# Transposed tokens in tiles of 512, streamed 512 at a time in three products

## The chip, the core and the metric

The kernel runs on one core of a Trainium2 chip. Its time is the device time of that core in microseconds. Three timed runs gave 2494.58, 2495.59 and 2495.97 us; the median is 2495.59 us. The engines are TensorE (PE, with its weight loads shown as PEld), VectorE (DVE), ScalarE (ACT), GpSimd (POOL) and SyncE (SP), which issues all DMAs here.

## The reference

One encoder layer is computed for two request groups with shared weights: S (512 tokens) and R (1024 tokens), both 1024 wide.

```
u = rmsnorm(x, mix_norm_g) @ w_in            # columns: z 512, xbc 1024, dt 16, q 512, k 512, v 512
ssd_out = ssd_mixer(z, xbc, dt)              # conv over tokens, two chunked scans, gate, norm
att_out = attention_mixer(q, k, v)           # dilated attention, three patterns
h = x + concat(ssd_out, att_out) @ w_out
h = h + memory_cross_attention(rmsnorm(h), rmsnorm(mem))      # 4 heads of 256, 256 memory tokens
hm = rmsnorm(h, mlp_norm_g)
return h + jnp.square(jax.nn.relu(hm @ mlp_w1)) @ mlp_w2      # 1024 -> 4096 -> 1024
```

All of it is float32. The kernel keeps that precision by splitting each operand of a large product into a high and a low part and summing three products.

## The kernel before

**Normed, transposed tokens.** Before each projection two token tiles of 128 are normed, transposed on PE into PSUM (`to_T`, L199) and written out by ACT as the high part `chi` (L205) and by DVE as the low part `clo` (L206). `at_pair` allots the two tiles, each 128 partitions by 8 slices `k` of the model width by 256 tokens. The pools `atA` and `atB` hold four such tiles each, so two pairs. `norm_T` and `to_T` fill a pair slice by slice.

**Products.** `mm3` (L181 to L183) issues three matmuls for one slice: high by high, low by high, high by low. In a matmul the first argument is the stationary operand, which is loaded as weights, and the second one streams. Two forms of product use the pairs:

- *Token-major* (`proj`): 128 tokens are stationary and 256 columns of a weight slab stream. Query, key and value, the gates, `w_out`, the memory's keys and values and the cross-attention's queries have this form. In the trace their matmuls read `mm<-whi,chi`: the streaming operand stands first.
- *Channel-major*: 128 columns of the weights are stationary and tokens stream, 256 at a time. This is `ch_major` in `w_in` (the 1024 conv channels), the time steps `steps` (32 columns of weights), and `up` in `mlp`, the feed-forward's first product. In the trace: `mm<-chi,whi`, `mm<-chi,wds` and `tp<-chi,whi`. A PSUM tile holds 512 tokens, so each of these runs 8 slices for the first pair of a block of 512 tokens and then 8 for the second.

**Feed-forward.** `up(fb)` makes 256 hidden channels (two groups `ft` of 128) for each block of 512 tokens: S has one block, R two. `down(fb)` multiplies them by 256 rows of `w2`, streaming 512 columns per matmul (`mm<-whi,hidh`), and adds to `h` on DVE (L947). There are 16 `fb`. `up(fb + 1)` is written ahead of `down(fb)`.

**Stages.** S: `w_in`, its scan `ssd`, its q, k and v. Then S's attention runs beside R's `w_in`, R's scan beside R's q, k and v, and R's attention beside S's `w_out`, cross-attention (`xattn`) and feed-forward. Last come R's `w_out`, cross-attention and feed-forward, with nothing beside them. `chain` holds the last three steps: `hn` norms a pair for the cross-attention and `hm` one for the feed-forward as soon as the pair's `h` is complete.

**What sets the order.** The source order isn't the order on the engines: a list scheduler places every instruction by its own estimate of when its operands are ready. On each engine the placed order is then fixed; an instruction whose operand isn't ready holds up those behind it. Dependences are kept by the parts of a tile that are read and written, and a pool's buffer is given on when its whole tile has been read.

Of the kernel before, what the change touches and what calls it, by code (L numbers as in the profile page):

```python
# [11 lines left out]
F32R = mybir.dt.float32r  # L12
# [8 lines left out]
KT = D // 128  # L21
# [63 lines left out]
def encoder(ctx: ExitStack, tc: tile.TileContext, I, y_p, y_s):  # L85
    nc = tc.nc
# [137 lines left out]
    def at_pair(atp):  # L224

        return tuple(atp.tile([128, KT, 256], F32R, name=n, tag="c8") for n in ("chi", "clo"))

    class Stream:
        def __init__(self, tag, x, mem, y, T):
            self.tag, self.x, self.mem, self.y, self.T = tag, x, mem, y, T  # L230
            self.nt = T // 128
            self.at, self.mixT, self.h, self.hn, self.hm = [], [], [], [], []
# [15 lines left out]
    def proj(w, hl, t):  # L248

        ps = mm_bank()[:, 0:256]  # L250
        (hi, lo), (wh, wl) = hl, w
        ts = slice(t * 128, t * 128 + 128)
        for k in range(KT):
            mm3(ps, hi[:, k, ts], lo[:, k, ts], wh[:, k, :], wl[:, k, :], k == 0, k == KT - 1)
        return ps


    def w_in_norm(st, pool, atp, b, first=None):

        for pr in range(2):  # L260
# [11 lines left out]
            st.at.append(at_pair(atp))  # L272
            norm_T(xs, *st.at[-1], "mix_norm_g", pool, more_banks if first else (tp_bank,))

    def w_in(st, pool, wx, first=False):
# [5 lines left out]
        def ch_major(ps, w, c, b):  # L281
            wh, wl = w
            cs = slice(c * 128, c * 128 + 128)
            for pr in range(2):
                hi, lo = at[b * 2 + pr]
                pp = ps[:, pr * 256:pr * 256 + 256]
                for k in range(KT):
                    mm3(pp, wh[:, k, cs], wl[:, k, cs], hi[:, k, :], lo[:, k, :], k == 0, k == KT - 1)
# [43 lines left out]
        def gate(c):  # L332
            w = slab(W_IN, OFF_Z + c * 256)
            for t in range(0, nt, 2):
                th = pool.tile([128, 512], F32, name="ev").rearrange("p (t c) -> p t c", t=2)
                for i in range(2):
                    ps = proj(w, at[t // 2], i)
# [6 lines left out]
        def steps(_):  # L344
# [8 lines left out]
            for b in range(nb):  # L353
                pd = mm_bank()
                for pr in range(2):
                    hi, lo = at[b * 2 + pr]
                    pp = pd[:32, pr * 256:pr * 256 + 256]
                    for k in range(KT):
                        nc.tensor.matmul(pp, wds[:, k, :], hi[:, k, :], start=k == 0, stop=False)
                        nc.tensor.matmul(pp, wds[:, k, :], lo[:, k, :], start=False, stop=k == KT - 1)  # L360
# [42 lines left out]
    def w_in_qkv(st, pool, rot, mid=None):  # L403
# [37 lines left out]
        for c in range(6):  # L441
            w = slab(W_IN, OFF_Q + c * 256)
            for t in range(0, nt, 2):
                hl = [pool.tile([128, 512], F32R, name="ev") for _ in range(2 if c < 4 else 1)]
                e = f(hl[-1]).rearrange("p (t c) -> p t c", t=2)
                for i in range(2):
                    ps = proj(w, st.at[t // 2], i)
# [279 lines left out]
    def memory_norm(pool, atp):  # L727
        for st in (S, R):
# [5 lines left out]
            st.mt = at_pair(atp)  # L734
            norm_T(xs, *st.mt, "mem_norm_g", pool)

    def memory(pool, late=None):
        for c in range(8):
# [3 lines left out]
            for st in (S, R):  # L742
                kf = pool.tile([128, 512], F32, name="ev").rearrange("p (m c) -> p m c", m=2)
                ss = pool.tile([128, 2], F32, name="kss", bufs=2)
                for mt in range(2):
                    ps = proj(w, st.mt, mt)
# [24 lines left out]
    def mix_T(st, pr, atp, banks=(tp_bank,)):  # L771
# [8 lines left out]
        st.mixT.append(at_pair(atp))  # L780
        to_T(xs, *st.mixT[-1], lambda k: gcol("ssd_norm_g", k), banks,
             lambda k: ident if k < 4 else back)

    def norm_h(st, pr, atp, gname, banks):
        hl = at_pair(atp)
# [265 lines left out]
```

## Time and profile before

| | |
|---|---|
| median of three timed runs | 2495.59 us |
| the profiled execution's own time | 2489.01 us |
| its span | 2487.2 us |
| PE busy | 2419.2 us (97%) |
| PEld busy | 2268.0 us (91%) |
| DVE, ACT, POOL busy | 1394.9, 951.3, 698.4 us |
| matmuls recorded | 17363 |
| mean granted TensorE clock | 0.993 of full speed |

Durations of matmuls overlap: one is shown from its start until its modelled end, while the next one has begun. So the rate of a stream is read from starts, not from durations. PE's idle time in a row is the time before an instruction in which no matmul was under way, with what ended it.

### The profile page before, as it was taken

The numbers are of one execution on the slowest core, as the hardware profiler recorded it, in microseconds if no ns is written. First come the engines' busy times: TensorE is split into PE (matmuls) and PEld (weight loads), VectorE is DVE, ScalarE is ACT, GpSimd is POOL, SyncE is SP. The second block draws the span as 40 slices with busy tenths as digits, with TensorE's granted clock in tenths as the row PEclk, the third lists the DMA queues.
The fourth block names the chain that finished last, engine by engine and source line by source line (L and its number), as shares of the span: only waits on it lengthen the run. The fifth ranks groups of instructions, "written<-read, shape, count | busy, mean of one in ns | idle before, by whom it ended". The sixth has DMA issues, their size and how long they took to land.

```text
span 2487.2 us, 43450 instructions
## 1 busy us (share of the span) xinstructions
PE 2419.2 (97%) x17363; PEld 2268.0 (91%) x17363; DVE 1394.9 (56%) x2750; ACT 951.3 (38%) x2153; POOL 698.4 (28%) x492
## 2 busy tenths in 40 slices
PE   8989999999989999999999999999999999999999
PEld 8889999889889988999989999999989989989897
DVE  6896775787735666655445636445544444443444
ACT  6655554455544655543222315334412212112120
POOL 3363112564422221314334211111222222122220
PEclk9999999999999999999999999999999999999999
DMA  5755443765567253425233411111111111101101
GB/s 187 243 192 181 126 146 106 225 201 189 187 194 214 85 150 98 116 83 184 92 101 103 170 52 35 52 60 44 35 52 35 51 52 51 52 35 52 52 35 68
DMA packets 224059, 272.59 MB, mean 110 GB/s; under 512 B 39634, under 2 KB 178160, under 8 KB 223856
## 3 DMA queue, kind: packets, MB, share of 16 engines
q1 hardware_dynamic: 223856, 269.80, 34.1%
q8 instruction: 137, 2.24, 0.4%
q14 instruction: 66, 0.54, 0.1%
HBM read 215.55 MB, written 54.20 MB: 108 GB/s over the span
## 4 chain that ended last, share of the span: by engine, by line
PE 79%; DMA 6%; DVE 6%; issue 3%; POOL 2%; ACT 2%; SPq 1%; POOLq 0%; DVEq 0%; ACTq 0%
PE mm L181 16%; PE mm L183 16%; PE mm L182 16%; PE tp L183 7%; PE tp L182 7%; PE tp L181 7%; PE mc L676 2%; PE ma L653 2%; PE mb L666 1%; DMA se<-acp 1%; DVE wlo L173 1%; PE tp L199 1%; DVE se L558 1%; POOL wlo L173 1%; DMA ak<-qkp 1%
## 5 line engine op out<-in xcount | busy, mean ns | idle before, releaser
L181 PE MATMUL mm<-whi,chi 128*128 128x256 f32 x1792 | 516.6, 289 | 2.1 <-ACT mm L749 1.2
L183 PE MATMUL mm<-whi,clo 128*128 128x256 f32 x1792 | 512.2, 287 | 0.0
L182 PE MATMUL mm<-wlo,chi 128*128 128x256 f32 x1792 | 511.3, 286 | 0.0
L947 DVE TENSOR_TENSOR h<-mm,h 128x512 f32<-128x512 f32 x384 | 262.2, 689 | 408.6 <-PE mm L183 408.6
L173 POOL TENSOR_TENSOR wlo<-raw,whi 128x1024 fp32r<-128x1024 f32 x120 | 296.9, 2474 | 601.4 <-ACT whi L172 585.9
L183 PE MATMUL tp<-chi,wlo 128*128 128x256 f32 x1440 | 408.4, 284 | 0.0
L182 PE MATMUL tp<-clo,whi 128*128 128x256 f32 x1440 | 407.9, 283 | 0.0
L181 PE MATMUL tp<-chi,whi 128*128 128x256 f32 x1440 | 405.6, 282 | 0.0
L172 ACT CAST whi<-raw 128x1024 fp32r<-128x1024 f32 x240 | 241.7, 1047 | 293.1 <-PE mm L183 168.1
L181 PEld LDWEIGHTS mm<-whi,chi 128*128 128x128 f32 x1792 | 341.1, 190 | 4.5 <-ACT chi L205 1.7
L182 PEld LDWEIGHTS mm<-wlo,chi 128*128 128x128 f32 x1792 | 341.0, 190 | 1.2 <-issue 0.2
L183 PEld LDWEIGHTS mm<-whi,clo 128*128 128x128 f32 x1792 | 339.9, 190 | 0.4
L173 DVE TENSOR_TENSOR wlo<-raw,whi 128x1024 fp32r<-128x1024 f32 x120 | 265.8, 2215 | 108.5 <-ACT whi L172 108.2
L181 PE MATMUL mm<-whi,hidh 128*128 128x512 f32 x768 | 303.1, 395 | 0.2 <-DVE h L947 0.2
L182 PE MATMUL mm<-wlo,hidh 128*128 128x512 f32 x768 | 302.6, 394 | 0.0
L183 PE MATMUL mm<-whi,hidl 128*128 128x512 f32 x768 | 302.3, 394 | 0.2 <-POOL hidl L932 0.2
L181 PEld LDWEIGHTS tp<-chi,whi 128*128 128x128 f32 x1440 | 272.5, 189 | 8.7
L183 PEld LDWEIGHTS tp<-chi,wlo 128*128 128x128 f32 x1440 | 271.7, 189 | 7.0
L182 PEld LDWEIGHTS tp<-clo,whi 128*128 128x128 f32 x1440 | 270.9, 188 | 6.5
L932 POOL TENSOR_TENSOR hidl<-hr,hidh 128x512 fp32r<-128x512 f32 x96 | 133.3, 1390 | 473.6 <-ACT hidh L931 473.6
L931 ACT CAST hidh<-hr 128x512 fp32r<-128x512 f32 x96 | 59.5, 620 | 320.6 <-PE mm L182 249.6
L183 PEld LDWEIGHTS mm<-whi,hidl 128*128 128x128 f32 x768 | 144.3, 188 | 34.0 <-POOL hidl L932 0.6
(283 smaller groups left out, 4398.3 us busy)
## 6 DMA issues: line engine op xcount, KB each, us to landing
raw<-in_mlp_w_dram SPq DMA_DIRECT2D x128, 512.0 KB
raw<-in_w_in_dram SPq DMA_DIRECT2D x48, 512.0 KB
qkp<-ev SPq DMA_DIRECT2D x32, 256.0 KB
se<-acp SPq DMA_DIRECT2D x16, 512.0 KB
raw<-in_xatt_wkv_dram SPq DMA_DIRECT2D x16, 512.0 KB
ak<-qkp SPq DMA_DIRECT2D x32, 256.0 KB
raw<-in_w_out_dram SPq DMA_DIRECT2D x16, 512.0 KB
raw<-in_xatt_wq_dram SPq DMA_DIRECT2D x16, 512.0 KB
```

The costliest lines, as they stand in the source:

```text
L172: nc.scalar.copy(hi[:, sl, :], raw)
L173: (nc.vector if s else nc.gpsimd).tensor_tensor(lo[:, sl, :], raw, f(hi[:, sl, :]), op=OP.subtract)
L181: nc.tensor.matmul(ps, lh, rh, start=start, stop=False)
L182: nc.tensor.matmul(ps, lh, rl, start=False, stop=False)
L183: nc.tensor.matmul(ps, ll, rh, start=False, stop=stop)
L199: nc.tensor.transpose(pt[:, k, t, :], xn[t][:, (2 * kp + k) * 128:(2 * kp + k + 1) * 128], units(2 * kp + k))
L558: nc.vector.scalar_tensor_tensor(w[:, h], cbm[:, 0, g], col[2], w[:, h], op0=OP.mult, op1=OP.add)
L653: nc.tensor.matmul(pq[:, i, :W], qu, ops[i][0][j], start=j == 0, stop=j == 1)
L676: nc.tensor.matmul(po[:, i * 64:i * 64 + 64], pT[:, i * nk + j, :], ops[i][1][j][:, rs], start=j == 0, stop=j == nk - 1)
L931: nc.scalar.copy(hh[:, ft], r)
L932: nc.gpsimd.tensor_tensor(hl[:, ft], r, f(hh[:, ft]), op=OP.subtract)
L947: nc.vector.tensor_tensor(h[t][:, cs], ps, h[t][:, cs], op=OP.add)
```

## The change

`at_pair` becomes `at_quad`: a tile now holds 512 tokens, in pools of two tiles where there were four, so the memory is the same. `norm_T` and `to_T` still work on two token tiles; `pair` hands them one half of a quad. `proj` takes its 128 tokens from the quad they lie in. `ch_major`, `steps` and `up` stream the quad's 512 tokens in one matmul where they streamed 256 twice. S's and R's normed memory share one quad. A quad's buffer is given on as a whole.

```
-    def at_pair(atp):
-
-        return tuple(atp.tile([128, KT, 256], F32R, name=n, tag="c8") for n in ("chi", "clo"))
+    def at_quad(atp):
+
+        return tuple(atp.tile([128, KT, 512], F32R, name=n, tag="c16") for n in ("chi", "clo"))
+
+    def pair(quad, pr):
+        sl = slice(pr % 2 * 256, pr % 2 * 256 + 256)
+        return tuple(x[:, :, sl] for x in quad)
...
-    def proj(w, hl, t):
+    def proj(w, quads, t):
 
         ps = mm_bank()[:, 0:256]
-        (hi, lo), (wh, wl) = hl, w
-        ts = slice(t * 128, t * 128 + 128)
+        (hi, lo), (wh, wl) = quads[t // 4], w
+        ts = slice(t % 4 * 128, t % 4 * 128 + 128)
...
     def w_in_norm(st, pool, atp, b, first=None):
 
+        st.at.append(at_quad(atp))
         for pr in range(2):
...
-            st.at.append(at_pair(atp))
-            norm_T(xs, *st.at[-1], "mix_norm_g", pool, more_banks if first else (tp_bank,))
+            norm_T(xs, *pair(st.at[-1], pr), "mix_norm_g", pool, more_banks if first else (tp_bank,))
...
         def ch_major(ps, w, c, b):
             wh, wl = w
             cs = slice(c * 128, c * 128 + 128)
-            for pr in range(2):
-                hi, lo = at[b * 2 + pr]
-                pp = ps[:, pr * 256:pr * 256 + 256]
-                for k in range(KT):
-                    mm3(pp, wh[:, k, cs], wl[:, k, cs], hi[:, k, :], lo[:, k, :], k == 0, k == KT - 1)
+            hi, lo = at[b]
+            for k in range(KT):
+                mm3(ps, wh[:, k, cs], wl[:, k, cs], hi[:, k, :], lo[:, k, :], k == 0, k == KT - 1)
...
-                for pr in range(2):
-                    hi, lo = at[b * 2 + pr]
-                    pp = pd[:32, pr * 256:pr * 256 + 256]
-                    for k in range(KT):
-                        nc.tensor.matmul(pp, wds[:, k, :], hi[:, k, :], start=k == 0, stop=False)
-                        nc.tensor.matmul(pp, wds[:, k, :], lo[:, k, :], start=False, stop=k == KT - 1)
+                hi, lo = at[b]
+                for k in range(KT):
+                    nc.tensor.matmul(pd[:32, :], wds[:, k, :], hi[:, k, :], start=k == 0, stop=False)
+                    nc.tensor.matmul(pd[:32, :], wds[:, k, :], lo[:, k, :], start=False, stop=k == KT - 1)
...
     def memory_norm(pool, atp):
-        for st in (S, R):
+        quad = at_quad(atp)
+        for i, st in enumerate((S, R)):
...
-            st.mt = at_pair(atp)
-            norm_T(xs, *st.mt, "mem_norm_g", pool)
+            st.mt = (quad, 2 * i)
+            norm_T(xs, *pair(quad, i), "mem_norm_g", pool)
...
-    def norm_h(st, pr, atp, gname, banks):
-        hl = at_pair(atp)
-        norm_T(st.h[2 * pr:2 * pr + 2], *hl, gname, banks=banks)
-        return hl
+    def norm_h(st, pr, quads, atp, gname, banks):
+        if pr % 2 == 0:
+            quads.append(at_quad(atp))
+        norm_T(st.h[2 * pr:2 * pr + 2], *pair(quads[-1], pr), gname, banks=banks)
...
                 for ft in range(2):
                     ps = tp_bank() if fb else mm_bank()
                     cs = slice(ft * 128, ft * 128 + 128)
-                    for pr in range(2):
-                        hi, lo = hm[b * 2 + pr]
-                        pp = ps[:, pr * 256:pr * 256 + 256]
-                        for k in range(KT):
-                            mm3(pp, wh[:, k, cs], wl[:, k, cs], hi[:, k, :], lo[:, k, :], k == 0, k == KT - 1)
+                    hi, lo = hm[b]
+                    for k in range(KT):
+                        mm3(ps, wh[:, k, cs], wl[:, k, cs], hi[:, k, :], lo[:, k, :], k == 0, k == KT - 1)
...
-    atA = open_pool(ctx, "atA", 4)
+    atA = open_pool(ctx, "atA", 2)
...
-        atB = open_pool(es, "atB", 4)
+        atB = open_pool(es, "atB", 2)
...
-        atB = open_pool(es, "atB2", 4)
+        atB = open_pool(es, "atB2", 2)
```

The remaining lines of the diff pass quads where pairs were passed (`gate`, `w_in_qkv`, `memory`, `mix_T`, `w_out`, `query`, `chain`).

How this moves instructions on PE is shown at two places. The first is the start of the program. Here `xn` is a normed tile of S's first pair and `xl__186`, `xl__188` the two of its second; `tp`, `ma`, `mb` are PSUM banks that transposes write, `mm` is one that products write. Before:

```order
L199 MATMUL mb<-ident,xn 128x128 x3
L181 MATMUL mm<-chi,whi 128x256
L182 MATMUL mm<-clo,whi 128x256
L181 MATMUL mm<-chi,whi 128x256
L182 MATMUL mm<-clo,whi 128x256
L199 MATMUL tp<-ident,xl__186 128x128
L199 MATMUL tp<-ident,xl__188 128x128
L199 MATMUL tp<-ident,xl__186 128x128
L199 MATMUL tp<-ident,xl__188 128x128
L183 MATMUL mm<-chi,wlo 128x256
```

Now:

```order
L199 MATMUL mb<-ident,xn 128x128 x3
L199 MATMUL tp<-ident,xl__186 128x128
L199 MATMUL tp<-ident,xl__188 128x128
L199 MATMUL tp<-ident,xl__186 128x128
L199 MATMUL tp<-ident,xl__188 128x128
L181 MATMUL mm<-chi,whi 128x512 x2
L199 MATMUL ma<-ident,xl__186 128x128
L199 MATMUL ma<-ident,xl__188 128x128
L199 MATMUL ma<-ident,xl__186 128x128
L199 MATMUL ma<-ident,xl__188 128x128
```

Before, 37 products of the first pair stand among the second pair's 16 transposes. Now two of 512 tokens and one of the time steps do, and the transposes have moved ahead of the rest.

The second place is on PE too, at the end of S's cross-attention, where its feed-forward's first product begins. `ma`, `mb` and `mc` here are steps of R's attention (scores, transposes, values), `xoh` and `xol` belong to the cross-attention's output product. Before:

```order
L183 MATMUL mm<-whi,xol 128x512
L199 MATMUL tp<-ident,xn 128x128
L181 MATMUL mm<-chi,whi 128x256
L182 MATMUL mm<-clo,whi 128x256
L183 MATMUL mm<-chi,wlo 128x256
L653 MATMUL ma<-ak,aq 128x256 x4
L181 MATMUL mm<-chi,whi 128x256
L182 MATMUL mm<-clo,whi 128x256
L183 MATMUL mm<-chi,wlo 128x256
```

Now:

```order
L183 MATMUL mm<-whi,xol 128x512
L199 MATMUL tp<-ident,xn 128x128 x4
L677 MATMUL mc<-avb,apT 128x64 x4
L667 MATMUL mb<-ident,asc 128x128 x4
L654 MATMUL ma<-ak,aq 128x256 x8
L199 MATMUL tp<-ident,xn 128x128
L677 MATMUL mc<-avb,apT 128x64 x4
L667 MATMUL mb<-ident,asc 128x128 x4
L199 MATMUL tp<-ident,xn 128x128 x7
L677 MATMUL mc<-avc,apT 128x64 x4
L667 MATMUL mb<-ident,asc 128x128 x4
L181 MATMUL mm<-chi,whi 128x512 x2
```

Before, 84 products of 256 tokens stand between the cross-attention's last product and the last transpose of S's second pair. Now 14 products of 512 tokens do, and one more group of value products (`mc`) and transposes (`mb`) of R's attention.

## Rows read from the trace of the kernel before

**Rows 1.** The page: busy time by engine; PE's granted clock in 40 slices

```profile
PE 2419.2 (97%) x17363; PEld 2268.0 (91%) x17363; DVE 1394.9 (56%) x2750; ACT 951.3 (38%) x2153; POOL 698.4 (28%) x492
...
PEclk9999999999999999999999999999999999999999
```

**Rows 2.** The chain that ended last, by engine

```profile
PE 79%; DMA 6%; DVE 6%; issue 3%; POOL 2%; ACT 2%; SPq 1%; POOLq 0%; DVEq 0%; ACTq 0%
```

**Rows 3.** By stage: stretch, PE, PEld, DVE, ACT, POOL busy, clock, DMA share, GB/s

```profile
13.00:79.00 66.00, 65.06 (x546) 64.10 (x546) 51.20 (x106) 37.65 (x66) 19.32 (x11) 1.00 0.57 176
79.00:200.00 121.00, 109.08 (x835) 105.19 (x835) 107.94 (x217) 71.11 (x169) 71.94 (x60) 0.96 0.66 215
200.00:1133.00 933.00, 892.81 (x7056) 861.58 (x7055) 595.57 (x1511) 476.31 (x1264) 298.57 (x227) 0.99 0.50 152
1133.00:2487.00 1354.00, 1347.93 (x8915) 1233.82 (x8914) 635.82 (x903) 358.68 (x644) 306.16 (x188) 1.00 0.19 66
```

**Rows 4.** PE in order of time (start us, us, operation): the feed-forward's streams

```profile
1177.79 0.40 PE L181 MATMUL mm<-whi,hidh 128*128 128x512 f32 x1
...
1245.54 0.40 PE L181 MATMUL mm<-whi,hidh 128*128 128x512 f32 x1
...
1780.94 0.28 PE L181 MATMUL tp<-chi,whi 128*128 128x256 f32 x1
...
1803.73 0.39 PE L181 MATMUL mm<-whi,hidh 128*128 128x512 f32 x1
...
2391.40 0.40 PE L181 MATMUL mm<-whi,hidh 128*128 128x512 f32 x1
...
2436.61 0.40 PE L181 MATMUL mm<-whi,hidh 128*128 128x512 f32 x1
...
2481.18 0.40 PE L183 MATMUL mm<-whi,hidl 128*128 128x512 f32 x1
```

**Rows 5.** The same view, R's `w_out`: 256 columns of weights stream

```profile
1427.42 0.36 PE L183 MATMUL mm<-whi,clo 128*128 128x256 f32 x1
...
1490.99 0.60 PE L199 MATMUL tp<-ident,xn 128*128 128x128 f32 x4
```

**Rows 6.** The same view, the start: first product, second pair's last transpose

```profile
13.08 0.58 PE L181 MATMUL mm<-chi,whi 128*128 128x256 f32 x1 [0.30 <-ACT whi L172]
...
20.77 0.27 PE L199 MATMUL mb<-ident,xl__188 128*128 128x128 f32 x1
```

**Rows 7.** R's conv channels: first product; the fourth pair's transposes

```profile
206.50 0.36 PE L181 MATMUL mm<-chi,whi 128*128 128x256 f32 x1
...
225.25 0.38 PE L199 MATMUL tp<-ident,xn 128*128 128x128 f32 x2
...
234.07 0.60 PE L199 MATMUL tp<-ident,xn 128*128 128x128 f32 x4
```

**Rows 8.** DVE in order of time: the fourth pair's second tile

```profile
224.98 0.75 DVE L220 TENSOR_SCALAR xn<-xn,rsr 128x1024 f32<-128x1024 f32 x1 [0.67 <-POOL rsr L190]
```

**Rows 9.** PE: S's feed-forward begins; R's attention; last transposes

```profile
1005.44 0.37 PE L181 MATMUL mm<-chi,whi 128*128 128x256 f32 x1
...
1011.56 0.60 PE L653 MATMUL ma<-ak,aq 128*128 128x256 f32 x3 [1.31 <-DMA ak<-qkp]
1011.99 1.00 PE L676 MATMUL mc<-avc,apT 128*128 128x64 f32 x8
...
1013.19 0.37 PE L182 MATMUL mm<-clo,whi 128*128 128x256 f32 x1
...
1020.96 0.60 PE L199 MATMUL tp<-ident,xn 128*128 128x128 f32 x4
```

**Rows 10.** ACT in order of time: the last high part of that pair

```profile
1022.63 0.47 ACT L205 ACTIVATE chi<-tp,cols 128x256 fp32r<-128x256 f32 x1 [0.55 <-DVE clo L206]
```

**Rows 11.** PE: R's feed-forward begins; first product after the transposes

```profile
1756.32 0.37 PE L181 MATMUL mm<-chi,whi 128*128 128x256 f32 x1
...
1766.86 0.36 PE L183 MATMUL mm<-chi,wlo 128*128 128x256 f32 x1
```

More of the change, by code (lines that the diff above doesn't have):

```diff
@@ L336, in gate @@
                 for i in range(2):
-                    ps = proj(w, at[t // 2], i)
+                    ps = proj(w, at, t + i)
                     nc.scalar.activation(th[:, i], ps, AF.Tanh, scale=0.5)
@@ L446, in w_in_qkv @@
                 for i in range(2):
-                    ps = proj(w, st.at[t // 2], i)
+                    ps = proj(w, st.at, t + i)
                     nc.scalar.copy(e[:, i], ps)
@@ L745, in memory @@
                 for mt in range(2):
-                    ps = proj(w, st.mt, mt)
+                    ps = proj(w, st.mt[:1], st.mt[1] + mt)
                     nc.scalar.copy(kf[:, mt], ps)
@@ L779, in mix_T @@
             xs.append(x)
-        st.mixT.append(at_pair(atp))
-        to_T(xs, *st.mixT[-1], lambda k: gcol("ssd_norm_g", k), banks,
+        if pr % 2 == 0:
+            st.mixT.append(at_quad(atp))
+        to_T(xs, *pair(st.mixT[-1], pr), lambda k: gcol("ssd_norm_g", k), banks,
              lambda k: ident if k < 4 else back)
-    def norm_h(st, pr, atp, gname, banks):
-        hl = at_pair(atp)
-        norm_T(st.h[2 * pr:2 * pr + 2], *hl, gname, banks=banks)
-        return hl
+    def norm_h(st, pr, quads, atp, gname, banks):
+        if pr % 2 == 0:
+            quads.append(at_quad(atp))
+        norm_T(st.h[2 * pr:2 * pr + 2], *pair(quads[-1], pr), gname, banks=banks)
     def w_out(st, hp, done):
@@ L797, in w_out @@
             for t in range(st.nt):
-                ps = proj(w, st.mixT[t // 2], t % 2)
+                ps = proj(w, st.mixT, t)
                 hs = st.h[t][:, c * 256:c * 256 + 256]
@@ L816, in query @@
             for t in range(2):
-                ps = proj(wq[c], st.hn[pr], t)
+                ps = proj(wq[c], st.hn, 2 * pr + t)
                 q = xk.tile([128, 256], F32, name="xq", bufs=nbuf)
@@ L971, in hn @@
         def hn(pr):
-            st.hn.append(norm_h(st, pr, pools[pr // 2], "xatt_norm_g", banks))
+            norm_h(st, pr, st.hn, pools[pr // 2], "xatt_norm_g", banks)
         def hm(pr):
-            st.hm.append(norm_h(st, pr, pools[pr // 2], "mlp_norm_g", banks))
+            norm_h(st, pr, st.hm, pools[pr // 2], "mlp_norm_g", banks)
         w_out(st, hp, hn)
```

## The prediction

> **What bounds the kernel now.** I read the page first: PE is busy 97% of the span, at 0.9 or more of its full clock in every slice [rows 1], and the chain that ended last is 79% PE [rows 2]. A busy PE isn't a PE at its peak, so I then cut the span by stage [rows 3]. From 1133 to 2487 us PE lacks 6 us of 1354: there the end is set by how fast PE takes its instructions, and a gain in that rate is a gain in time. From 13 to 1133 us it lacks 53 us, and from 79 to 200 us DVE is busy 89%: a saved matmul may there turn into waiting. The last view, PE in order of time, gives the rates by starts.
>
> **The rate of a stream.** In R's feed-forward one `fb` holds 192 products of 256 tokens (first product) and 96 of 512 columns (second). The same place in the pattern is met at 1803.73 and, 13 `fb` later, at 2391.40 [rows 4]: 587.67 / 13 = 45.205 us per `fb`. How that splits I bound from two sides. The last 192 products of 512 columns run alone, from 2436.61 to 2481.18, the start of the last one: 44.57 / 191 = 0.2333 us each. That leaves (45.205 - 96 x 0.2333) / 192 = 0.1188 for a small one, which the 192 small ones alone from 1780.94 to 1803.73 bear out, 22.79 / 192 = 0.1187 [rows 4]. The other side: of all steps between 1803.73 and 2391.40, each given to the product that starts it, 2496 small ones average 0.1197 and 1248 large ones 0.2315 us. So a merged pair saves 2 x 0.1188 - 0.2333 = 4.3 ns at one end and 2 x 0.1197 - 0.2315 = 7.9 at the other, 2 to 3%. I take the middle, 0.2324 us for a large one and 6 ns for a pair. It can't be much, because the columns streamed stay the same.
>
> The Trainium skill ("TensorE: Matmul & The Clock Gate", section "Back-to-back issue gap") puts a warm step at the columns divided by 2.4 GHz plus a fixed 2.5 ns. By that a merged pair saves 2.5 ns, 7 us over all pairs where the rows give 12 to 23. The trace doesn't agree: 0.1187 and 0.2333 us stand 12 and 20 ns above the bare streaming time. What would follow from it is the third rival.
>
> **The change part by part.** Durations are those of the profiled execution (2489.01 us, 1.8 us more than its span). The sum is a difference and is carried over to the median of the runs shown, 2495.59 us, which is 6.6 us above.
>
> *Feed-forward, first product.* 4608 products become 2304. R: an `fb` then has 192 large ones, 192 x 0.2324 = 44.62 us in place of 45.205: -0.58 us, 16 times, -9.3 us. S: three `fb` take 1245.54 - 1177.79 = 67.75 us [rows 4], 22.58 each, and become 96 x 0.2324 = 22.31: -0.27 us, 16 times, -4.4 us. Together -13.7 us; with 0.2333 it is -9.4, with 0.2315 it is -17.9. Most of it lies after 1133 us, where nothing but PE sets the pace [rows 3], so I count all of it.
>
> *Conv channels and time steps.* 8 groups x 3 blocks x 48 products: 1152 become 576. At 4.3 to 7.9 ns that is -2.5 to -4.6 us; where DVE sets the pace it can come to nothing. I take -3.0. The time steps' 96 products become 48, worth 0.3 us at the same price; I leave them out.
>
> *The wait added.* A product over a quad needs both halves of slice `k`. What PE did on the first pair while the second was normed and transposed now has to wait, and behind a waiting product PE's whole queue stands, with attention steps that ACT and DVE wait for. This happens at three places. At each I compare what stands on PE ahead of the second pair's last transpose.
>
> Start of the program: the first product starts at 13.08 us, the second pair's last transpose at 20.77 [rows 6]. 37 products of the first pair stand between them, 37 x 0.119 = 4.4 us of PE. Now 3 large ones do, 0.7 us. From 13 to 79 us PE is 98.6% busy [rows 3], so work put off is late: +3.7 us (0 to 4.4, since the transposes also move forward).
>
> R's conv channels: the first block's product starts at 206.50, the fourth pair's first transpose at 225.25 [rows 7]. Between them stand 134 products, 96 of the first block and 38 of the third pair. The 38 can't run there any more, 38 x 0.119 = 4.5 us. The fourth pair is normed at 224.98 + 0.75 us [rows 8], so PE gets there early and waits; S's attention fills a part. From there to 234.07 the old order has 35 products, 4.2 us, the new one 20 large ones, 4.6 us: nothing more is lost. +2.0 us (0 to 4.5).
>
> S's feed-forward: it begins at 1005.44, and the second pair's last transposes start at 1020.96 [rows 9]. 84 products of the first pair stand between, 84 x 0.119 = 10.0 us. Now 14 large ones do, 3.3 us, and one more `mc` and `mb` of R's attention, 1013.19 - 1011.99 = 1.2 us [rows 9]. The 1.3 us in which PE waited there for a DMA (`ak`, [rows 9]) fall under the same stand. 10.0 - 3.3 - 1.2 - 1.3: +4.2 us (0 to 10.0).
>
> R's feed-forward has the same wait for its second block, between 1756.32 and 1766.86 [rows 11]. But there 46 products of the first block stand in the new order, 46 x 0.2324 = 10.7 us: the cover is as long as the stretch. 0.
>
> *Release by quads.* The memory's tiles, and those for the cross-attention after `w_out`, get their buffers later by two token tiles' products, 48 x 0.119 = 5.7 us at most. A token-major product costs the same, 535 in 63.57 us [rows 5]. At each such time other projections or R's attention stand on PE, so I cost it at 0; without that cover it would be 5.7 us once, at S's `w_out`.
>
> *The order.* The scheduler places everything anew. From 1133 us on the order is that of before in larger pieces. Up to there PE's 53 us of waiting [rows 3] can shift either way; I give that +/- 4 us and no mean.
>
> Sum: -13.7 - 3.0 + 3.7 + 2.0 + 4.2 = -6.8 us. The profiled execution would go from 2489.0 to 2482.2, the median from 2495.6 to **2488.8 us**.
>
> **Rivals.**
>
> 1. *The waits cost nothing* (chance 0.24). R's attention fills PE's stands, and the work put off is done in gaps that exist anyway. For: the 53 us of gaps up to 1133 us. Against: at the start and near 1005 us PE is nearly full. -13.7 - 3.0 = -16.7: 2478.9 us.
>
> 2. *S's feed-forward stands until its second pair is whole* (0.08). That pair's norms share ACT and DVE with R's attention: its last high part is written at 1022.63 + 0.47 us [rows 10]. If PE's queue stands from 1005.44 until then, R's attention behind it stands too: 17.7 us. With the bounds of the start, 4.4, and of the conv channels, 4.5: -16.7 + 17.7 + 8.9 = +9.9, 2505.5 us. It decides from about 13 us at this one place, where the sum passes +5. Against: the new order puts `mc`, `mb` and `ma` ahead of the products, and a slice's products need that slice alone.
>
> 3. *Only a small fixed part is saved* (0.10). The large products seen so far stream weights; those of the first product would stream tokens, and no row shows 512 tokens streamed. If a merged pair saved 2.5 ns, below the rows' end of 4.3, 2880 pairs give -7.2, and with the waits' +9.9 the sum is +2.7: 2498.3 us, no measurable change. By the skill's rule named above this is what comes out. Against: 256 tokens and 256 columns of weights stream at one rate, 0.1187 and 63.57 / 535 = 0.1188 us [rows 4, 5].
>
> **How the numbers follow.** The forecast has 0.58. Its own range is 2481 to 2496 us (the pair's saving +/- 4 us, the waits +/- 4, the order +/- 4, not all at once). The range that holds 8 in 10 reaches down past rival 1 by a little luck in the order, 2476, and up over the forecast with the lower saving and rival 3, 2498; it leaves out rival 2. A difference under 0.2%, 5.0 us, can't be told from none. Faster is then below 2490.6: 0.36 of the forecast's 0.58 and 0.23 of rival 1's 0.24, 0.59 together. The forecast's upper part (0.20) and most of rival 3 and the rest of rival 1 (0.10) make 0.30 for the same. Rival 2 and small upper ends of the others make 0.11 for slower.
>
> **What would show it.** Equal places of two `fb` should lie 44.6 us apart in R's feed-forward and 22.3 in S's; at 45.0 or above rival 3 holds. At the start PE's idle time from 13 to 21 us should grow by 3 to 4 us. Where S's feed-forward begins, the list of waits should name PE waiting for `chi`, `clo` or the transposes' sources by some 4 us. The forecast is wrong if those waits pass 13 us, or if PE's waiting up to 1133 us moves by more than 10 us away from these places, which would be the scheduler's doing.

## The result and the profile after

The changed kernel takes 2514.13 us (median of 4 runs, 2511.93 to 2521.41), the kernel before 2495.78 on the same chip (2494.58 to 2496.01): a ratio of 1.0082, 95% interval 1.0068 to 1.0097. It is slower by 18.4 us, where 2488.8 us and a gain of 6.8 were predicted; 2514 lies outside the range. The profiled execution took 2511.93 us, its span is 2509.9.

The page of the kernel after has these lines where before had [rows 1]:

```profile
PE 2418.0 (96%) x14435; PEld 2130.5 (85%) x14435; DVE 1399.0 (56%) x2750; ACT 951.5 (38%) x2153; POOL 693.8 (28%) x492
...
PEclk9998999999999999999999999999999999999999
```

PE executes 2928 products fewer, as the change says (2304 + 576 + 48), and is busy for as long as before. Its busy time also holds the stretches at a lower clock, and they have grown: the mean granted clock is 0.985 in place of 0.993, and one slice now has a clock below 0.9. The stages, in the place of [rows 3] (same columns; the bounds moved to where the work of that stage stands now):

```profile
13.00:83.00 70.00, 67.25 (x339) 54.99 (x339) 55.03 (x112) 39.11 (x69) 20.40 (x11) 1.00 0.55 165
83.00:217.00 134.00, 113.96 (x835) 109.97 (x836) 102.83 (x214) 71.65 (x169) 71.22 (x61) 0.91 0.59 190
217.00:1166.00 949.00, 895.68 (x6344) 829.91 (x6344) 603.85 (x1492) 470.38 (x1237) 299.73 (x227) 0.97 0.50 151
1166.00:2510.00 1344.00, 1337.05 (x6904) 1132.39 (x6903) 633.07 (x921) 363.05 (x669) 300.02 (x186) 1.00 0.20 66
```

The second stage, with the same 835 PE instructions as before, takes 134 us in place of 121: PE idles 20.0 us of it in place of 11.9, and the clock is 0.91 in place of 0.96. The third takes 949 in place of 933, at 0.97 in place of 0.99. The last is 10 us shorter. PE in order of time shows why, at equal places of the feed-forwards' pattern [rows 4]:

```profile
1257.62 0.39 PE L181 MATMUL mm<-whi,hidh 128*128 128x512 f32 x1
...
1369.01 0.39 PE L181 MATMUL mm<-whi,hidh 128*128 128x512 f32 x1
...
1890.86 0.39 PE L181 MATMUL mm<-whi,hidh 128*128 128x512 f32 x1
...
2425.34 0.39 PE L181 MATMUL mm<-whi,hidh 128*128 128x512 f32 x1
```

In S five `fb` take 111.39 us, 22.28 each (before 22.58, predicted 22.31); in R twelve take 534.48, 44.54 each (before 45.205, predicted 44.62). That is 16 x 0.30 + 16 x 0.665 = 15.5 us gained. So the whole loss, some 34 us against the gain, arises ahead of that. The places named in the prediction look like this now; first the start [rows 6], then the first products of R's conv channels, of S's feed-forward and of R's [rows 7, 9, 11]:

```profile
14.69 0.45 PE L199 MATMUL tp<-ident,xl__186 128*128 128x128 f32 x1 [1.75 <-DVE clo L206]
...
16.82 1.22 PE L181 MATMUL mm<-chi,whi 128*128 128x512 f32 x2 [1.04 <-ACT chi L205]
...
20.61 0.42 PE L199 MATMUL mb<-ident,xl__188 128*128 128x128 f32 x1
...
223.19 0.47 PE L181 MATMUL mm<-chi,whi 128*128 128x512 f32 x1
...
1044.68 0.71 PE L181 MATMUL mm<-chi,whi 128*128 128x512 f32 x2
...
1790.20 0.48 PE L181 MATMUL mm<-chi,whi 128*128 128x512 f32 x1
```

13.08 has become 16.82, 206.50 has become 223.19, 1005.44 is 1044.68, 1756.32 is 1790.20. The first product starts 3.7 us later, as much as the prediction gave for the start; then 13 us go between 71 and 223 us, where no product of the change runs, and 22 more up to 1045 (some 10 of them, as the last section shows, because this execution of before was one of the quickest). The list of PE's waits (us in total, times, longest) had at its top before:

```profile
PE tp L433 <- DVE ev L428: 11.9, 7, 3.2
...
PE mb L573 <- DVE syo L575: 5.1, 2, 4.4
PE ma L653 <- DVE aband L655: 4.3, 4, 2.7
```

Now:

```profile
PE tp L434 <- DVE ev L429: 9.1, 4, 4.5
PE ma L654 <- DVE aband L656: 8.2, 2, 8.0
...
PE mm L181 <- ACT ev L449: 7.5, 4, 4.4
PE mb L574 <- DVE syo L576: 7.4, 4, 2.8
PE mm L181 <- ACT chi L205: 5.8, 3, 2.8
```

The head steps of q and k (`ev`), the attention (`aband`) and the scan (`syo`) stand there in both; single waits are longer now, up to 8.0 us. Of the 5.8 us for `chi` only the 1.04 at the start is at a place of the prediction.

### The profile page after: what moved, and what is told of

The parts are those of the page before. It is cut to its first block, busy times and chain, and to the rows that moved or that the text cites. A ratio compares the mean times of both kernels' runs of the same rounds, so it can differ in the third digit from the quotient of the medians.

```text
span 2509.9 us, 37578 instructions
## 1 busy us (share of the span) xinstructions
PE 2418.0 (96%) x14435; PEld 2130.5 (85%) x14435; DVE 1399.0 (56%) x2750; ACT 951.5 (38%) x2153; POOL 693.8 (28%) x492
## 4 chain that ended last, share of the span: by engine, by line
PE 61%; DVE 1%; DMA 1%; ACT 1%; issue 1%; POOL 0%; SPq 0%; ACTq 0%; DVEq 0%; POOLq 0%
PE mm L181 12%; PE mm L183 12%; PE mm L182 12%; PE tp L183 6%; PE tp L182 6%; PE tp L181 6%; PE mc L677 1%; PE mb L667 1%; PE ma L654 1%; PE tp L199 1%; DVE wlo L173 0%; ACT whi L172 0%; PE tp L825 0%; PE ma L182 0%; PE ma L183 0%
## 5 line engine op out<-in xcount | busy, mean ns | idle before, releaser
L183 PE MATMUL tp<-chi,wlo 128*128 128x512 f32 x720 | 284.3, 395 | 0.0
L181 PE MATMUL tp<-chi,whi 128*128 128x512 f32 x720 | 283.9, 394 | 0.0
L182 PE MATMUL tp<-clo,whi 128*128 128x512 f32 x720 | 283.8, 394 | 0.0
L181 PEld LDWEIGHTS mm<-whi,hidh 128*128 128x128 f32 x768 | 144.4, 188 | 35.3 <-DVE h L948 2.4
L182 PEld LDWEIGHTS mm<-wlo,hidh 128*128 128x128 f32 x768 | 144.5, 188 | 32.7
L183 PEld LDWEIGHTS tp<-chi,wlo 128*128 128x128 f32 x720 | 135.4, 188 | 31.6
```

The source lines that it names most:

```text
L181: nc.tensor.matmul(ps, lh, rh, start=start, stop=False)
L182: nc.tensor.matmul(ps, lh, rl, start=False, stop=False)
L183: nc.tensor.matmul(ps, ll, rh, start=False, stop=stop)
```

## Experiments

Two theories stood after this. **A**: the products gain what was predicted, and the loss is the scheduler's new order up to 1045 us. **B**: the products of 512 themselves do it, because each waits for a whole tile of tokens and PE's queue stands behind it. Differences below are between medians of one kernel and of the kernel before on the same chip; ratios have their 95% interval.

To hold the order still, a table of places is added behind the traced program. It chains the instructions of each engine by issue order alone, which adds no wait of its own:

```diff
+def in_order(tc):
...
+        for a, b in zip(place[:-1], place[1:]):
+            tc.add_manual_dep(ins[b], ins[a].name, info, reason="order")
...
         encoder(tc, args, outs[0][0], outs[1][0])
+        in_order(tc)
```

### Order and products crossed (E1, E2, E5)

E1 is the changed kernel with the table of the old order:

> The changed kernel's own products and tiles, with a table that chains the instructions of each engine in the order of the kernel before (a product of 512 stands where the second of its two halves stood; ACT, DVE, POOL and SP are in the old order word for word). Theory A, the loss is the scheduler's new order up to 1045 us: without that order the gain is there, -15 in the feed-forwards and -3 in the conv channels, less up to 10 for work that stands later at the three places of the prediction: 2479 to 2489 us, and R's first conv product near 207 to 212 us where the changed kernel has it at 223. Theory B, the loss is in the products themselves (a product of 512 waits for a whole tile, and PE's queue with it): the waits come along with the products, R's first conv product stays near 220 and S's feed-forward starts 30 us or more later than before: 2505 to 2515 us.

Measured 2510.20 us, +14.3 (1.0051, 1.0035 to 1.0067), inside theory B's expectation. Theory A is not borne out in this form: the old order did not bring the gain. But its products of 512 stood in lumps.

E2 is the kernel before with the changed kernel's order:

> The reverse: the products of 256 and the tiles by pairs of the kernel before, chained in the order of the changed kernel (where that has 24 products of 512 for a bank, 48 of 256 stand in their places, the first pair's ahead of the second's). Theory A: the order alone makes it slow, and the small products cost their 15 to 18 us more on top, less what a product of the first pair no longer waits for (up to 8): 2520 to 2532 us. Theory B: with small products the waits are gone, and it comes back to the kernel before, 2492 to 2502 us.

Measured 2522.12 us, +26.2 (1.0101, 1.0085 to 1.0117), inside theory A's expectation. The new order is slow without a single product of 512 or tile of 512 in it: theory B alone can't be right either.

E5 repeats E1 with another table, in which a product of 512 stands at the second of two neighbouring old places, or later where the second pair's slice isn't yet written:

> As the first kernel (the changed kernel's products and tiles, every engine chained in the order of before), but a product of 512 stands where the second of the two neighbouring places of its bank was, so the 24 products are spread over the 48 old places, and only as far back as the second pair's slice is written (one block of R's time steps stays as it was). Theory A2, where the products stand in PE's order makes the time (in the first kernel they stood in lumps at the end of each bank's stretch, with the attention's and scan's steps ahead of them uncovered): the 16 us lost by 320 us and the 10 lost near 1005 us go, and it comes to 2479 to 2489 us. Theory B, a product of 512 costs its wait wherever it stands: 2503 to 2511 us again.

Measured 2497.41 us, +0.5 (0.9999, 0.9988 to 1.0010), between the two expectations. Where the same products stand in the same surroundings is worth 13 us (E1 to E5). With the old order the new products gain nothing and lose nothing; the changed kernel's own order costs 17.9 us on top (+18.4 against +0.5).

### Which products bring what (E3, E4, E6, E11, E9)

E3 streams 512 in the feed-forward alone, E4 in the projections alone, E6 nowhere (tiles of 512 with two halves of 256):

```diff
-            hi, lo = at[b]
-            for k in range(KT):
-                mm3(ps, wh[:, k, cs], wl[:, k, cs], hi[:, k, :], lo[:, k, :], k == 0, k == KT - 1)
+            for pr in range(2):
+                hi, lo = pair(at[b], pr)
+                pp = ps[:, pr * 256:pr * 256 + 256]
+                for k in range(KT):
+                    mm3(pp, wh[:, k, cs], wl[:, k, cs], hi[:, k, :], lo[:, k, :], k == 0, k == KT - 1)
```

(E3 has this in `ch_major` and the like in `steps`, E4 the like in `up`, E6 all three.)

> Tiles of 512 tokens throughout, but the channel-major projections and the time steps stream them in two halves of 256; only the feed-forward's first product streams 512. Its instructions stand as in the kernel before up to where S's feed-forward begins (near 1005 us). Theory A: front as before, the feed-forwards' gain of 15 whole, less 3 to 5 at the start of S's feed-forward: 2483 to 2487 us, the fastest so far. Theory B, in the form that every product of 512 brings its wait: a good part of the gain goes at the start of the two feed-forwards, 2488 to 2496 us.

> The counterpart: channel-major projections and time steps stream 512, the feed-forward's first product two halves of 256. Its instructions stand as in the changed kernel up to where S's feed-forward begins (near 1045 us). Theories A and B alike put the whole loss ahead of that place, so it keeps the loss and lacks the gain of 15, with 3 to 5 back at the start of S's feed-forward: 2524 to 2530 us. If the loss came from the feed-forwards after all it would be near 2496.

> Tiles of 512 tokens, every product over them in two halves of 256: the instructions of all engines stand in the order of the kernel before, word for word; only the tiles are released as a whole. All theories: no difference, 2493 to 2499 us. If the release by 512 tokens cost something, up to 6 us at each of its places, it would be 2500 us or more. Since nothing else differs, its profile also shows how far two executions of one order lie apart up to 1005 us.

E3 2487.53 us, -8.4 (0.9967, 0.9954 to 0.9980); E4 2520.68, +24.8 (1.0096, 1.0080 to 1.0112); E6 2495.88, -1.0 (0.9996, 0.9985 to 1.0007). The release of tiles by 512 costs nothing. E3 lies just outside theory A's expectation: the feed-forwards keep 8 of their 15.5 us. E4, a little under its own, puts the rest of the loss into the projections and what the scheduler does around them.

E11 leaves 256 in the first `fb` too, so that no product there has to wait for the second pair:

```diff
+                    for n in range(1 if fb else 2):
+                        ns = slice(0, 512) if fb else slice(n * 256, n * 256 + 256)
```

> Only the feed-forwards stream 512, and only from their second fb on; no chain. The order is that of before up to the first fb of S's feed-forward. All theories: the 15/16 of 15 us are gained, and the 6 us that the kernel with 512 in all fb lost at the start of S's feed-forward come back: 2480 to 2484 us, the fastest version without a chain. If that 6 was not a wait for the second pair it stays at 2487.

Measured 2481.96 us, -16.0 (0.9944, 0.9931 to 0.9956), as expected: 7.6 us ahead of E3, whose loss is the wait in the first `fb` of S's feed-forward. By the count explained below E3 loses 7 us between 1000 and 1025 us, E11 under 1.

E9 has 512 everywhere except where the second pair is late (E11's edit, the projections' first slab and the time steps by halves), in the old order:

```diff
-            for k in range(KT):
+            for n in range(1 if whole else 2):
+                ns = slice(0, 512) if whole else slice(n * 256, n * 256 + 256)
...
-                    ch_major(ps, w, c, b)
+                    ch_major(ps, w, c, b, sl > 0)
```

> Products of 512 as in the changed kernel except where the second pair is late: the first weight slab of the channel-major projections (S and R), the time steps and the first fb of both feed-forwards stream two halves of 256. Chained in the order of the kernel before, each product of 512 at the second of two neighbouring places of its bank; none had to move back for a slice not yet written. Theory A (the gain is in the rate, the loss in waits for the second pair at the three places and in the new order): both losses are gone, the gain is left, 15/16 of 15 us in the feed-forwards and 2 to 3 in the projections: 2477 to 2482 us, 0.9925 to 0.9945 of before. Theory B (a product of 512 costs PE's neighbours something wherever it stands, by the coarser gaps that it leaves to attention and scan): half of the 17 or more is lost, 2488 us or above.

Measured 2480.46 us, -17.5 (0.9938, 0.9925 to 0.9951), the lowest median of all. The gain in rate is there; what the projections add to E11's 16.0, 1.5 us, can't be told from nothing. E5 is 18.0 us behind. It differs from E9 by streaming 512 at the three places too (and, with them, in the time steps, the first slab of R's second block and R's first `fb`), and by the products that had to move back. The waits at the three places cost that: the count below puts most of it there.

What such a wait is, the same three stretches show (columns as in [rows 3]) in E6, in E5 and in E9: the start, R's conv channels, S's feed-forward.

```profile
13.00:30.00 17.00, 16.84 (x127) 16.05 (x128) 12.56 (x34) 11.24 (x24) 6.20 (x5) 1.00 0.70 214
200.00:250.00 50.00, 49.36 (x427) 48.72 (x426) 28.15 (x83) 29.61 (x76) 12.12 (x12) 1.00 0.54 168
1000.00:1050.00 50.00, 47.41 (x363) 44.48 (x362) 31.63 (x78) 26.23 (x61) 15.53 (x10) 1.00 0.46 118
```

E5, 512 everywhere:

```profile
13.00:30.00 17.00, 12.61 (x49) 9.53 (x50) 12.63 (x35) 10.60 (x24) 6.32 (x5) 0.80 0.53 158
200.00:250.00 50.00, 43.89 (x260) 39.26 (x259) 24.73 (x71) 23.41 (x59) 12.67 (x10) 0.90 0.49 151
1000.00:1050.00 50.00, 46.31 (x256) 39.38 (x256) 30.98 (x85) 25.22 (x68) 8.52 (x8) 0.90 0.43 113
```

E9, 512 except there:

```profile
13.00:30.00 17.00, 16.13 (x132) 15.56 (x133) 12.23 (x34) 11.67 (x25) 6.43 (x6) 1.00 0.71 218
200.00:250.00 50.00, 49.71 (x429) 48.70 (x428) 30.34 (x92) 29.23 (x75) 9.88 (x11) 1.00 0.55 167
1000.00:1050.00 50.00, 47.86 (x296) 42.64 (x295) 32.56 (x72) 25.68 (x54) 20.38 (x11) 0.97 0.50 127
```

PE's idle time grows from E6 to E5 by 4.2 + 5.5 + 1.1 = 10.8 us. The prediction gave 3.7 + 2.0 + 4.2 = 9.9 to the waits, so the sum is close, the parts aren't. What it left out is the third column from the end, the granted clock: 0.80, 0.90 and 0.90 in place of 1.00, another 17 x 0.20 + 50 x 0.10 + 50 x 0.10 = 13.4 us of work lost at most (a lower clock costs nothing while PE idles). Together that is more than the 18.0 us between the medians; by the count below, part comes back later. In the order of time (start us, us, operation) PE at R's conv channels in E5:

```profile
229.15 0.60 PE L667 MATMUL mb<-ident,asc 128*128 128x128 f32 x4
233.45 0.63 PE L654 MATMUL ma<-ak,aq 128*128 128x128 f32 x4 [3.70 <-DVE aband L656]
234.51 0.41 PE L199 MATMUL tp<-ident,xn 128*128 128x128 f32 x2 [0.43 <-DVE amx L659]
235.08 1.97 PE L677 MATMUL mc<-avb,apT 128*128 128x64 f32 x8 [0.17 <-DVE rst L188]
236.85 1.06 PE L667 MATMUL mb<-ident,asc 128*128 128x128 f32 x4
...
239.61 0.78 PE L181 MATMUL mm<-chi,whi 128*128 128x512 f32 x1
```

And in E9:

```profile
225.54 1.00 PE L681 MATMUL mc<-avb,apT 128*128 128x64 f32 x8
226.38 0.61 PE L671 MATMUL mb<-ident,asc 128*128 128x128 f32 x4
226.74 0.36 PE L181 MATMUL mm<-chi,whi 128*128 128x256 f32 x1
226.94 0.60 PE L199 MATMUL tp<-ident,xn 128*128 128x128 f32 x4
227.29 0.64 PE L658 MATMUL ma<-ak,aq 128*128 128x128 f32 x4
```

E9 has products of the third pair between attention steps; E5 has none left, and waits 3.70 us for DVE's part of an attention step. Here the wait is not at a product for `chi` or `clo`, where the prediction looked for it. At the start it is of that kind: in E5 PE waits 1.7 us there for `clo` at a transpose and 1.5 and 1.3 us for `chi` and `clo` at products. At S's feed-forward its longest wait is 2.7 us for the DMA of `ak` (1.7 in E6). After the 3.70 us at R's conv channels the same `mc` takes 1.97 us in place of 1.00, `mb` 1.06 in place of 0.61, a product of 512 0.78 in place of the 0.39 of other rows: the granted clock is 0.50 from 237 to 245 us, the lower of its two levels, 1.2 GHz. The Trainium skill ("TensorE: Matmul & The Clock Gate", section "Why this matters for your kernels") warns that idle gaps of PE between bursts bring the half rate back; this trace agrees, 3.70 us of waiting followed by doubled times.

### The scheduler's order (E7, E8, E10, E12 to E16)

E10 is E9 without the table. E7 and E8 exchange DVE and POOL for a weight slab's low parts in the kernels before and after; E15 does so in E10:

```diff
-            (nc.vector if s else nc.gpsimd).tensor_tensor(lo[:, sl, :], raw, f(hi[:, sl, :]), op=OP.subtract)
+            (nc.gpsimd if s else nc.vector).tensor_tensor(lo[:, sl, :], raw, f(hi[:, sl, :]), op=OP.subtract)
```

> The kernel before with one change that alters no amount of work: of a weight slab's two halves DVE now takes the low part of the first and POOL that of the second (before, the other way round). The scheduler places everything anew from the first slab on. Theory A: the order it happens to find moves the time by more than the 5 us that can be told apart, either way: below 2489 or above 2501 us, most of it up to 1045 us. Rival C, that orders of these products are all about alike and only the products of 512 upset them: 2491 to 2501 us.

> The same exchange of DVE and POOL in the changed kernel. Theory A: the loss belongs to the order that the scheduler happened to find, so against the kernel before with the same exchange it is another number than +18, anywhere between -20 and +25, with the gain of 15 in the feed-forwards in it. Rival C: the products of 512 upset any order, and the changed kernel is again 12 to 25 us behind its own counterpart.

> The same products without the chain: the scheduler places them. Theory A: no product waits for a late pair any more, and what is left against the chained kernel is the scheduler's order alone, up to 20 us: 2479 to 2500 us, with the difference arising before 1005 us. Rival C (the order is only bad because of the waits): as the chained one within 5 us, 2477 to 2486.

E7 2500.43 us, +3.5 (1.0016, 1.0004 to 1.0029): inside rival C's expectation, so this draw alone doesn't bear theory A out. E8 2504.53, +7.6 (1.0037, 1.0024 to 1.0051), so the change costs 4.1 us in that pair and 18.4 in the first, where rival C asked for 12 to 25. E10 2498.62, +0.7 (1.0007, 0.9997 to 1.0018), inside theory A's expectation and 18.2 behind E9 with the same products. E9 and E10 differ by the chain alone; in E7, E8 and E14 to E16 the exchange also changes which engine makes a part, so their differences aren't the order's alone.

E12 streams 512 in R's projections alone, E13 (`first` in place of `not first`) in S's alone:

```diff
-                    ch_major(ps, w, c, b)
+                    ch_major(ps, w, c, b, not first)
```

> Only R's channel-major projections stream 512 (S's, the time steps and the feed-forwards 256), no chain; order as before up to R's first conv product (206 us). Theory A: from there on the scheduler's order is another. If the places at R's conv (9 us at its start, 10 us near 370, both seen in three orders with 512 there) come from 512 in R's projections, it is 2505 to 2515 us; if the bad order starts with S's projections, the wait at the start of R's conv alone is left, less a gain of 2: 2496 to 2505 us.

> Only S's channel-major projections stream 512 (R's, the time steps and the feed-forwards 256), no chain. Theory A: the wait at the program's start, 4 to 5 us, and the scheduler's order from 75 to 225 us, which lost 4 to 13 us wherever 512 stood in S's projections, but not the 10 us near 370, which came with R's: 2498 to 2512 us. Rival D, that the order from 75 us on is luck and has nothing to do with S's products: as before plus the 4 to 5 us of the start, within 3.

E12 2503.44 us, +5.5 (1.0030, 1.0020 to 1.0039), inside the lower expectation, that the wait at the start of R's conv channels alone is left; E13 2523.34, +26.9 (1.0112, 1.0094 to 1.0129), 11 us more than theory A's upper end.

E14 and E16 exchange ACT and DVE for the copies of the attention weights, in the kernel before and in E10:

```diff
-                if u0 % 4:
+                if not u0 % 4:
                     nc.scalar.copy(pTf[:, :2 * W], pt[:, :2 * W])
```

> The kernel before with another change that alters no amount of work: of the copies of transposed attention weights ACT takes the even ones and DVE the odd ones (before, the other way round). A third order for products of 256. If orders of 256 are alike (E7 was 3.5 us behind), 2492 to 2502 us; if the order is luck in either direction, off by 8 us or more.

> The kernel with 512 everywhere but in the first blocks (no chain), with DVE and POOL exchanged for a slab's low parts as in E7: a second order that the scheduler finds for these products. If its orders for products of 512 are worse than for 256 as a rule, it again lacks 12 to 20 us of the chained kernel's gain, 2492 to 2504 us against 2500 of its counterpart with 256; if the first one was bad luck it is 2483 to 2490.

> The same with ACT and DVE exchanged for the copies of the attention weights: a third order for these products. As a rule worse: 2492 to 2504 us, with fewer score products of S's attention (about 68 where orders for 256 have 81 to 84) by R's last conv product; luck: 2478 to 2490.

E14 2505.63 us, +9.2 (1.0039, 1.0023 to 1.0054), worse than expected for orders of 256; E15 2488.24, -8.2 (0.9967, 0.9956 to 0.9979), in the range that was given for luck; E16 2517.73, +21.3 (1.0086, 1.0070 to 1.0102), above both ranges. Against E9 the three orders found for one set of products cost 18.2, 9.3 and 38.8 us; the three found for 256 cost 0, 3.5 and 9.2 against the kernel before. Luck is large, and the draws for 512 were the worse ones. Each beside the kernel with 256 and the same exchange, the three are at +0.7 (E10 and before), -11.7 (E15 and E7) and +12.1 us (E16 and E14).

Where it is lost, a count shows. For each profiled execution I added up the columns that PE's instructions stream, in order of time, and read off when the sum reaches the share that E6 has reached at a given time. The table gives the delay against E6 in us, good to about 1 us; the last column counts the records of S's score products (`ma`) between R's first conv product and its last. (The 81 to 84 that E16's expectation names for orders of 256 are 80 when counted record by record. E13's profiled execution is 6 us above its median.)

```
E6's time       75    200    225    350    375   1000   1025   1300   2300    ma
before        -0.5   -1.6   -2.3   -3.5   -3.4  -10.0  -10.2  -10.9  -11.3    80
E9            -1.2   -2.6   -3.1   -3.3   -3.5   -6.3   -4.4   -8.8  -17.9    80
E5            +4.6   +8.3  +17.3  +12.3  +12.1   +7.3  +15.2   +9.5   -0.5    80
E1            +2.6   +5.7  +13.5  +12.4  +12.2   +8.6  +17.5  +19.7  +13.2    80
after         +3.8  +15.3  +25.7  +17.3  +26.3  +21.3  +27.7  +24.0  +15.0    68
E2            +4.0   +9.6  +19.8  +11.9  +21.6  +17.6  +25.3  +24.7  +24.0    68
E10           +2.3  +11.5  +12.4   +6.7  +16.4  +16.0  +14.9  +10.7   +1.7    68
E16           +3.7  +11.8  +12.3   +9.2  +18.6  +19.6  +23.7  +27.1  +17.9    68
E12           +0.7   -0.2   +5.8   -4.3   +4.5   +4.5   +4.6   +3.8   +2.9    68
E13           +2.1  +19.6  +19.3  +23.2  +22.9  +30.4  +29.7  +30.2  +29.8    80
E14           +0.7   -0.1   -0.9   -3.0   +1.5   -9.2   -6.0   +3.0   +2.1    72
```

Two places stand out. From 75 to 200 us the orders of the scheduler with 512 in S's projections lose 8 to 18 us (after, E10, E16, E13; E15 5, E8 6), in a stage without such products: S's scan and its q, k, v. (E7, an order for 256, loses 11.5 there too and gets it back by 1000 us.) And from 350 to 375 us every order with 68 or 72 score products in R's conv stretch loses 4.5 to 11 us (also E15 and E8 with 68), every one with 80 nothing. Most of this second loss is a lead given back: from 225 to 350 us the same orders gain 2 to 10 us on E6. From 225 to 375 as a whole they are between 1.3 us ahead (E12) and 6.3 behind (E16), so what the kernel after lacks at 375 us (26.3) it already lacks at 225 (25.7). Near 360 us the conv products have run out ahead of S's attention, which they cover. The kernel after, in stretches of 10 us (columns as in [rows 3]):

```profile
360.00:370.00 10.00, 10.00 (x72) 9.35 (x71) 7.23 (x12) 4.72 (x8) 2.40 (x1) 1.00 0.36 93
370.00:380.00 10.00, 2.62 (x22) 2.41 (x21) 9.93 (x19) 2.22 (x4) 3.02 (x2) 0.89 0.56 180
380.00:390.00 10.00, 9.37 (x64) 9.27 (x65) 4.84 (x21) 4.73 (x17) 0.61 (x1) 0.77 0.23 80
```

PE waits 8.0 us for `aband` and comes back at a lower clock. DVE is busy 9.93 of the 10 us: steps of R's conv channels (`cacc`) stand in its order ahead of `aband`. E10's list of PE's waits from 345 to 385 us has the same:

```profile
PE ma L658 <- DVE aband L660: 6.8, 1, 6.8
PE mb L671 <- DVE aband L660: 0.9, 1, 0.9
```

E9, with E10's products in the old order, has no wait of PE there at all. In E12 and E14 the longest wait between 330 and 400 us is 1.8 and 1.2 us.

## Why the prediction was wrong

The step that failed is "The order": "The scheduler places everything anew ... Up to there PE's 53 us of waiting can shift either way; I give that +/- 4 us and no mean." With the products held and only the order changed it is +17.9 us (after against E5), and +9 to +39 in three other draws (E10, E15, E16 against E9). This term alone turns the sum over; in E5, where the order is held, 2497.41 us lies inside the predicted range. The 53 us of waiting became 76 (13 to 1166 us by the stages above), far more than +/- 4. The prediction had named this sign: PE's waiting moves by over 10 us away from its three places. From 13 to 21 us it grew by 1.8 us only (0.9 to 2.7), and where S's feed-forward begins the list of waits names neither `chi` nor `clo`. That the trace of before was already packed to 98% in some stretches by one particular order was a reason to expect a new draw to be worse rather than better; the runs don't show that as a rule.

- *The rate of a stream*: right. 0.665 and 0.30 us per `fb` where 0.58 and 0.27 were predicted, so 6.9 and 6.4 ns per merged pair; 15.5 us in place of 13.7. E9's -17.5 holds this and the projections' share (predicted for its products: 13.7 x 15/16 + 3.0 x 3/4 = 15.1). Rival 3, 2.5 ns a pair, is out.
- *The wait added*: right in place, too small by half: 9.9 us predicted, 18.0 measured (E5 against E9; with the 1.6 us of gain that E5 has over E9 at these places, 19.6). The idle time's sum, 10.8, came near by luck: by place it is 4.2, 5.5 and 1.1 us where 3.7, 2.0 and 4.2 were given, and 5.5 is above the bound of 4.5. The stretch at half clock behind each wait had no term. The 84 products counted at S's feed-forward are also too many: in the trace of before 68 products stand ahead of the second pair's last transpose, and at most 48 of them (2 groups x 8 slices x 3) are the first pair's. With 68 the term is 8.1 - 3.3 - 1.2 - 1.3 = 2.3 us in place of 4.2. By the count above (E5 less E9) the start has 5.8 us by 75 us and 10.9 by 200, R's conv channels add 9.5 by 225, of which 4.8 come back by 350, and S's feed-forward adds 6.0. R's feed-forward added nothing, as predicted: some 8 us behind E6 at 1700 us in E5, some 5 at 1900, when the merged products have begun to gain.
- *Release by quads*: nothing, as predicted (E6).
- *Rival 1* (waits cost nothing) is what E9 and E11 make true by leaving the late places at 256. *Rival 2* (S's feed-forward stands until its pair is whole, 17.7 us) didn't happen: 7 to 8 us against E6 there in E3 and E5.
- *The base*: the profiled execution of before was one of the quickest. E6 has its order word for word, and its profiled execution takes 2499.37 us against 2489.01. This moves no term of the difference, but a comparison of two single traces up to 1000 us is uncertain by as much.

Open is why the orders found for products of 512 come out worse. That fewer attention steps then stand among R's conv products is seen in E12's count (68 against 80, R's projections alone changed), but E12 as a whole loses 5.5 us, and what in the scheduler's choice costs the time up to 225 us isn't shown. E14 and E7 show losses in orders for products of 256 as well. Three draws for 256 and five for 512 don't give a distribution; that the order of before is simply a good one, which any new draw is likely to miss, isn't excluded.

## What to carry to other kernels

Merge products where both halves are there anyway, and leave the block that meets its data fresh in the smaller size: from the second `fb` on, the merge alone brings 0.9944 [0.9931, 0.9956] without touching anything else. Where a scheduler places the program anew, hold the old order by a chain before judging an edit (E1 and E5 show that the places given to the merged products matter too, 13 us): here the draw of the order moved the time by 18 us with nothing else changed (E9 and E10), as much as the edit's own worth, and by up to 39 together with an exchange of engines. An order worth keeping can be written in. A wait of PE in a nearly full stretch is to be priced twice, once for the idle time and once for the stretch at half clock that can follow it.

## What was not expected of the hardware

Two executions of one order differ by 10 us up to 1000 us, and hardly after that (before and E6 in the table). In stretches of 50 us up to 1100 PE idles 61.7 and 63.7 us in them, but the clock's shortfall, the sum of 50 us x (1 - granted clock), is 15.0 and 23.0 us: about the same waits are followed by the lower clock in one execution and not in the other. Before and E6 from 150 to 200 us:

```profile
150.00:200.00 50.00, 46.24 (x367) 44.58 (x366) 45.18 (x93) 26.03 (x62) 32.44 (x29) 1.00 0.54 175
150.00:200.00 50.00, 46.46 (x355) 44.52 (x355) 45.99 (x93) 26.46 (x64) 30.92 (x28) 0.97 0.54 175
```

This is one pair of traces. In the kernel after PE idles 84.3 us up to 1100, and the clock's shortfall is 36.5 us.
